# Two parts of a hybrid decoder's mixer trade places: sparse heads first and in pairs, MLA and stick-breaking beside half of the output projection

## The chip, the cores and the metric

One core of a Trainium2 chip (trn2) runs the kernel. The metric is the device time of one execution in microseconds, as the median of several runs. Lower is better.

## The reference

A decoder trunk of two layers on 256 tokens of width 1024, in float32. Each layer computes:

```python
x = x + 0.5 * swiglu(rmsnorm(x, g1), w_gate1, w_up1, w_down1)        # 2816 wide
h = rmsnorm(x, g_mix) @ w_in                                        # 2354 columns, cut into head groups
o_mla = mla_attention(...)              # 6 heads, low-rank q and kv, rotary key, causal softmax
o_nsa = nsa_attention(...)              # 6 query heads in 2 groups: compressed, selected, window branches
o_sb  = stick_breaking_attention(...)   # 4 heads, no softmax, strictly causal
x = x + concat(o_mla, o_nsa, o_sb) @ w_out                          # 1024 x 1024
x = x + 0.5 * swiglu(rmsnorm(x, g2), w_gate2, w_up2, w_down2)
```

and a last RMSNorm follows. With 256 tokens the selected and the window branch of the sparse attention (NSA) see all earlier tokens, so each is a plain causal softmax with keys and values of its own. The compressed branch has 15 keys and values per group, made by a two-layer network with GELU from overlapping runs of 32 tokens. A sigmoid gate weighs each branch.

## The kernel before

The residual stream lies feature-major in `xT`, 128 features on the partitions by 256 tokens. Weight matrices stay float32 in HBM. They come in as `raw` tiles (four buffers), and `split` (L86) makes two halves of each, `wh` on ScalarE and `wl = raw - wh` on VectorE, in a format that TensorE multiplies in one pass. A product is three matmuls of halves (`mm3`, L222, and the inner loops of `ffn` and `project`). The products of the attentions are full float32; each of those shows as two records in the trace.

`mix(l)` (L742) is the stage between the two feed-forward networks. Its parts are Python generators whose `yield`s cut them into steps. `weave(g, h, n)` (L403) traces all steps of `g` with `n` steps of `h` after each, and `mixed` (L414) traces several generators in turn. The order of tracing is a priority: the compiler's scheduler takes it, but lets work that is ready by its own estimate pass work that isn't. On the chip each engine then issues strictly in that order.

In `mix`, `project` (L370) computes one block of columns of the input projection into two PSUM banks. The order is: A (MLA's latents; statistics of the norm behind it), SQ (stick-breaking queries and keys) with `latents` (L510) woven in, SV, `up_project` (L525, MLA's queries, keys and values from the latents). Then come K, Q and V, the sparse attention's columns, woven with MLA (`latent_attention`, L605), stick-breaking (L556) and, from Q on, `compressed` (L625). After that `sparse_attention` (L720) runs by itself, one head after the other: `softmax_pair` (L460) computes the scores of the two branches, the probabilities and their transposes, and `pv` (L505) multiplies them with the values. Last comes the output projection in two halves of its columns (`out_half`, L835), all 1024 rows of `w_out` in each.

A head has 64 features, so a score matmul uses 64 rows of the array and a value matmul 64 columns. The six query heads lie as two groups on partitions 0 to 63 and 64 to 127. The PSUM banks have four tags of two each: `a0`, `a1`, `g0`, `g1`.

In `compressed` the first layer of the small network is 16 matmuls per branch with 30 rows of result (L650 to L655), all to the same partitions.

Of the kernel before, what the change touches and what calls it, by code (L numbers as in the profile page):

```python
# [10 lines left out]
F32 = mybir.dt.float32  # L11
# [8 lines left out]
T = 256  # L20
# [11 lines left out]
NB = 15  # L32

# [9 lines left out]
def _shape_constants():  # L43
# [13 lines left out]
    return tab, np.concatenate([tri, -np.ones((128, 128), np.float32), bd.reshape(128, 128)], 1)  # L57
# [3 lines left out]
def trunk(ctx, tc, a, out):  # L61
# [64 lines left out]
    mats = con.tile([128, 384], F32, name="mats")  # L126
    negtri, negones, bdm = mats[:, 0:128], mats[:, 128:256], mats[:, 256:384].rearrange("p (j d) -> p j d", j=2)
    cosn, sinn = tab[:, :, 0:16], tab[:, :, 16:32]
# [16 lines left out]
    for m in (maskc, masks, kcbd, hidp, pcm):  # L145
        POOL.memset(m, 0.0)
# [43 lines left out]
    def norm_in(n, l, d):  # L190
# [6 lines left out]
        else:  # L197
            s = sb.tile([128, T], F32, name="sq", tag="sq", bufs=2)
            ACT.activation(s, xT[:, d], AF.Square)
# [151 lines left out]
    def finish(xt2, t, c, sm):  # L351
        """Final norm: the gain first, the token's scale once both halves are summed."""
        s = slice(c * 512, c * 512 + 512)
        y = xt2[:, t, s]
        o = sb.tile([128, 768], F32, name="o", tag="PT", bufs=2)[:, :512]
# [14 lines left out]
    def project(l, c0, c1, tag):  # L370
        """One block of columns of the input projection, as a list of steps and its two banks."""
# [31 lines left out]
    def weave(g, h, n):  # L403
        """All steps of g, with n steps of h after each."""
# [9 lines left out]
    def mixed(*gens):  # L414
        """The steps of several generators in turn."""
# [44 lines left out]
    def softmax_pair(tag, q, k, res, gate=None):  # L460
        """Causal softmax of two score streams; the probabilities transposed: [key, stream, query]."""
# [11 lines left out]
        P = sb.tile([128, 768], F32, name="P", tag="P", bufs=2)  # L473
# [3 lines left out]
        for i, p, x, n in ((1, p1, x1, 256), (0, p0, x0, 128)):  # L477
# [6 lines left out]
            if gate is not None:  # L484
                DVE.tensor_tensor(f[:, i], f[:, i], gate[:, i], op=OP.mult)
# [13 lines left out]
        pt = sb.tile([128, 768], F32, name="PT", tag="PT", bufs=2)  # L499
# [5 lines left out]
    def pv(po, j, v, pt, first, last):  # L505
        rows = slice(64 * j, 64 * j + 64)
        mm(po[rows, 0:256], v[0], pt[0], first, False)
        mm(po[rows, 128:256], v[1], pt[1], False, last)

    def latents(l, A, ch, cl):  # L510
        """Transposes of the latents, with their gains, as exact halves."""
        for b0, nb in ((0, 2), (2, 1)):
# [5 lines left out]
            for b in range(nb):  # L518
                g = gam("mla_q_norm", l, b) if b0 == 0 else gam("mla_kv_norm", l, 0)
                pb = p[:, b * T:b * T + T]  # L520
                ACT.activation(ch[:, b0 + b], pb, AF.Copy, scale=g)
                DVE.scalar_tensor_tensor(cl[:, b0 + b], pb, g, ch[:, b0 + b].bitcast(F32), op0=OP.mult, op1=OP.subtract)
            yield

    def up_project(l, A, ch, cl, lr, qm, km, vm):  # L525
# [6 lines left out]
        for t in range(2):  # L532
            s = slice(t * 128, t * 128 + 128)
            q, k = qm[t], km[t]
            for c in range(2):
                p = bank("g%d" % c)[:, :288]
                f = slice(c * 288, c * 288 + 288)
                for kk in range(2):
                    mm(p, ch[:, kk, s], wuq[kk][0][:, f], kk == 0, False)
                    mm(p, ch[:, kk, s], wuq[kk][1][:, f], False, False)  # L540
                    mm(p, cl[:, kk, s], wuq[kk][0][:, f], False, kk == 1)
                evac(c, q[:, 3 * c:3 * c + 3].rearrange("p h d -> p (h d)"), p, lr[:, t:t + 1])
            for c in range(2):
                p = bank("g%d" % c)[:, :384]
                f = slice(c * 384, c * 384 + 384)
                mm(p, ch[:, 2, s], wkv[0][:, f], True, False)
                mm(p, ch[:, 2, s], wkv[1][:, f], False, False)
                mm(p, cl[:, 2, s], wkv[0][:, f], False, True)
# [7 lines left out]
    def stick_breaking(SQ, SV):  # L556
# [30 lines left out]
        for h in range(4):  # L587
# [12 lines left out]
            pv(po, h % 2, [SV[:, t, h * 64:h * 64 + 64] for t in range(2)], (at[:, 0:256], at[:, 256:384]), True, True)  # L600
# [4 lines left out]
    def latent_attention(qm, km, vm):  # L605
        for pr in range(3):
# [13 lines left out]
            for s in range(2):  # L620
                pv(po, s, [vm[:, t, 2 * pr + s] for t in range(2)], pts[0][s], True, True)
# [3 lines left out]
    def compressed(l, NQ, kv):  # L625
        """Keys and values of the compressed branch, on the diagonals of kcbd and kv."""
# [322 lines left out]
```

## Time and profile before

| | |
|---|---|
| median of 3 runs | 1097.53 us (1097.26 to 1099.15) |
| span of the profiled execution, first to last instruction | 1095.3 us |
| TensorE busy | 1072.1 us (98%), 8023 matmul records |
| VectorE, ScalarE, GpSimd busy | 62%, 49%, 9% |
| mean granted TensorE clock | 0.981 |
| HBM traffic | 160 GB/s over the span |

The page gives no device time of the profiled execution beside its span; the median of the runs stands for it. Engines are named PE (TensorE matmul), PEld (its weight loads), DVE (VectorE), ACT (ScalarE), POOL (GpSimd). A record's duration in a timeline reaches into the next one's, since matmuls are pipelined; the distance between two starts is what a matmul takes from the stream.

### The profile page before, as it was taken

The page shows a single profiled execution, that of the slowest core. Times are in us where ns is not written, and L with a number is a line of the kernel's source. Part 1 is how long each engine was busy: PE and PEld are TensorE (multiplying, and loading weights), DVE is VectorE, ACT ScalarE, POOL GpSimd, SP SyncE. Part 2 cuts the span into 40 slices and gives each one's busy share as a digit, 9 for nine tenths or more (in the row PEclk, how much of TensorE's full clock was granted, in tenths as well). Part 3 has the DMA queues.
Part 4 walks back from the last instruction along what each step waited for, and adds up shares of the span by engine and source line. Part 5 has one row for each costly group of instructions (what it writes and reads, how often), then busy time and mean ns, then how long its engine had stood idle before and what let it go on. Part 6 is the DMA issues. An engine that isn't in the chain of part 4 may idle for free.

```text
span 1095.3 us, 19386 instructions
## 1 busy us (share of the span) xinstructions
PE 1072.1 (98%) x8023; PEld 1008.0 (92%) x8023; DVE 684.3 (62%) x1088; ACT 535.7 (49%) x906; POOL 99.6 (9%) x171
## 2 busy tenths in 40 slices
PE   7999999999999999999999999999999999999996
PEld 7999999888868999999999999998887699999996
DVE  6666666765655766666686666667656466666664
ACT  5544444655444544444464444447645455444443
POOL 2000000322211100000020000003411220000001
PEclk9999999999969999999999999999998799999999
DMA  9646455373402456464555646553633035546441
GB/s 293 222 156 230 151 197 185 108 221 111 154 1 78 158 189 208 144 226 168 179 169 178 221 141 216 182 171 113 214 122 111 1 116 192 190 157 230 158 151 39
DMA packets 127974, 176.65 MB, mean 161 GB/s; under 512 B 4119, under 2 KB 106765, under 8 KB 127885
## 3 DMA queue, kind: packets, MB, share of 16 engines
q1 hardware_dynamic: 127392, 174.82, 47.3%
q8 instruction: 63, 1.03, 0.4%
q10 hardware_dynamic: 492, 0.59, 0.2%
q14 instruction: 27, 0.21, 0.1%
HBM read 174.34 MB, written 1.05 MB: 160 GB/s over the span
## 4 chain that ended last, share of the span: by engine, by line
PE 45%; DVE 2%; POOL 1%; ACT 1%; issue 1%; POOLq 0%; DVEq 0%
PE bkg L286 22%; PE bka L84 18%; PE bkg L84 3%; DVE wl L92 1%; DVE xl L193 0%; PE bkg L494 0%; PE bkg L612 0%; POOL rt L448 0%; PE bkg L496 0%; PE bkg L498 0%; POOL rt L449 0%; DVE xT L345 0%; DVE xt L335 0%; ACT wh L91 0%; POOL qm L451 0%
## 5 line engine op out<-in xcount | busy, mean ns | idle before, releaser
L91 ACT ACTIVATE wh<-raw 128x1024 fp32r<-128x1024 f32 (+4 forms) x332 | 339.0, 1025 | 426.9 <-PE bkg L286 203.5
L92 DVE TENSOR_TENSOR wl<-raw,wh 128x1024 fp32r<-128x1024 f32 (+4 forms) x332 | 394.1, 1191 | 185.5 <-ACT wh L91 178.9
L286 PE MATMUL bkg<-xl,wh 128*128 128x256 f32 x1392 | 390.3, 280 | 1.3 <-DVE xl L193 1.3
L286 PE MATMUL bkg<-xh,wh 128*128 128x256 f32 x1392 | 390.3, 281 | 0.7 <-ACT wh L91 0.7
L286 PE MATMUL bkg<-xh,wl 128*128 128x256 f32 x1392 | 389.4, 280 | 0.8 <-DVE wl L92 0.8
L286 PEld LDWEIGHTS bkg<-xl,wh 128*128 128x128 f32 x1392 | 262.1, 188 | 2.4 <-DVE xl L193 1.7
L286 PEld LDWEIGHTS bkg<-xh,wh 128*128 128x128 f32 x1392 | 262.1, 188 | 1.9 <-ACT wh L91 0.9
L286 PEld LDWEIGHTS bkg<-xh,wl 128*128 128x128 f32 x1392 | 262.0, 188 | 1.0 <-DVE wl L92 1.0
L84 PE MATMUL bka<-hh,wl 128*128 128x256 f32 x528 | 149.1, 283 | 0.0
L84 PE MATMUL bka<-hh,wh 128*128 128x256 f32 x528 | 148.9, 283 | 0.2
L84 PE MATMUL bka<-hl,wh 128*128 128x256 f32 x528 | 149.0, 283 | 0.0
L84 PEld LDWEIGHTS bka<-hh,wh 128*128 128x128 f32 x528 | 100.5, 191 | 0.8 <-ACT hh L308 0.8
L84 PEld LDWEIGHTS bka<-hh,wl 128*128 128x128 f32 x528 | 100.8, 191 | 0.0
L84 PEld LDWEIGHTS bka<-hl,wh 128*128 128x128 f32 x528 | 100.7, 191 | 0.0
L200 POOL TENSOR_TENSOR ss<-ss,sq 128x256 f32<-128x256 f32 x35 | 29.5, 844 | 599.4 <-issue 362.8
L300 DVE TENSOR_TENSOR t<-bkg,rb 128x256 f32<-128x256 f32 x88 | 37.4, 424 | 55.1 <-PE bkg L286 53.3
L84 PE MATMUL bka<-wh,xh 128*128 128x384 f32 (+4 forms) x192 | 68.5, 357 | 0.0
L303 DVE TENSOR_TENSOR t<-bkg,rb 128x256 f32<-128x256 f32 x88 | 37.3, 424 | 47.3 <-PE bkg L286 47.3
L84 PE MATMUL bka<-wh,xl 128*128 128x384 f32 (+4 forms) x192 | 66.4, 346 | 0.0
L84 PE MATMUL bka<-wl,xh 128*128 128x384 f32 (+4 forms) x192 | 66.3, 346 | 0.0
L440 ACT ACTIVATE P<-bka,st 128x256 f32<-128x256 f32 (+1 forms) x72 | 29.4, 415 | 31.7 <-PE bkg L498 14.4
L305 DVE TENSOR_TENSOR t<-t,t 128x256 f32<-128x256 f32 x88 | 37.4, 425 | 9.1 <-DVE t L303 0.5
(233 smaller groups left out, 1286.9 us busy)
## 6 DMA issues: line engine op xcount, KB each, us to landing
raw<-in_ffn_w_down_dram SPq DMA_DIRECT2D x44, 1024.0 KB, 5.1
raw<-in_ffn_w_gate_dram SPq DMA_DIRECT2D x43, 1024.0 KB, 5.8
raw<-in_ffn_w_up_dram SPq DMA_DIRECT2D x43, 1024.0 KB, 5.2
raw<-in_w_out_dram SPq DMA_DIRECT2D x16, 512.0 KB, 4.3
raw<-in_w_in_dram SPq DMA_DIRECT2D x8, 768.0 KB, 4.2
raw<-in_w_in_dram SPq DMA_DIRECT2D x4, 1024.0 KB, 5.4
raw<-in_w_in_dram SPq DMA_DIRECT2D x4, 832.0 KB, 4.5
raw<-in_w_in_dram SPq DMA_DIRECT2D x4, 804.0 KB, 5.5
```

What stands on the lines that cost most here:

```text
L84: PE.matmul(o, l, r, start=start, stop=stop, skip_group_check=True)
L91: ACT.activation(hv, src, AF.Copy)
L92: DVE.tensor_tensor(lv, src, hv.bitcast(F32), op=OP.subtract)
L200: POOL.tensor_tensor(state["ss"], state["ss"], s, op=OP.add)
L286: args[0](*args[1:], **flags)
L300: DVE.tensor_tensor(gn, pg[:, :T], rb, op=OP.mult)
L303: DVE.tensor_tensor(un, pu[:, :T], rb, op=OP.mult)
L305: DVE.tensor_tensor(h, gn, un, op=OP.mult)
L440: state["last_exp"] = ACT.activation(*args, **kw).ins
```

## The change

- The projections come in the order K, Q, V, A, SQ, SV. K and Q run bare, `compressed` is woven into V, and its rest, the transposes of the sparse rows and `sparse_attention` are one chain (`nsa`) woven into A, SQ, SV and `up_project`.
- `sparse_attention` takes a head of either group together: their score matmuls alternate between the two row halves, into a bank each; their value matmuls alternate between the column halves (`pv` now takes a list of heads). The gates and all scaling of the probabilities are applied on VectorE and GpSimd.
- The first layer of the compression writes to four groups of 32 partitions in turn, and a matmul with a 0/1 matrix (`sel32`) adds the four and turns the result.
- The output projection is cut by its rows: the sparse heads' three blocks (`out_sparse`) run first, for the second half of columns (added to `xT` at once) and then for the first, with MLA and stick-breaking woven in; the other five blocks follow (`out_late`). The sparse heads' rows of `w_out` are loaded in pieces of 64 rows.
- The ScalarE table for exp and log is loaded at the start of `mix` instead of behind A's squares.

```diff
@@ compressed
-            ph = bank("g1")[:30, :128]
             for j in range(16):
-                mm(ph, R[:, j].rearrange("p g b -> p (g b)"), w1[:, j], j == 0, j == 15)
+                c = slice(32 * (j % 4), 32 * (j % 4) + 32)
+                mm(ph[c], Rk[:, j], w1[:, j], j < 4, j >= 12)
...
-            PE.transpose(p[:, :30], hr[:30], ident[:30, :30])
+            mm(p[:, :32], hr, sel32, True, True)
@@ pv
-    def pv(po, j, v, pt, first, last):
-        rows = slice(64 * j, 64 * j + 64)
-        mm(po[rows, 0:256], v[0], pt[0], first, False)
-        mm(po[rows, 128:256], v[1], pt[1], False, last)
+    def pv(po, heads, first, last):
+        rows = [slice(64 * j, 64 * j + 64) for j in range(2)]
+        for j, (v, pt) in heads:
+            mm(po[rows[j], 0:256], v[0], pt[0], first, False)
+        for j, (v, pt) in heads:
+            mm(po[rows[j], 128:256], v[1], pt[1], False, last)
@@ sparse_attention
+        def scores(rr, t):
+            n = 128 * (t + 1)
...
+            X = [bank("a1") for _ in range(2)]
...
+            for g in range(2):
+                mm(xs[g][:, :, 128 * t:128 * t + 128], identb, maskc, True, False)
+            for s in range(2):
+                for g in range(2):
+                    mm(xs[g][:, s], nT[rr][grp[g], 128 * t:128 * t + 128], nT[3 + s][grp[g], 0:n], False, True)
...
+            for g in range(2):
+                POOL.tensor_tensor(p[g], p[g],
+                                   f[:, g].rearrange("p (s o) -> p s o", o=1).to_broadcast([128, 2, n]), op=OP.mult)
...
+        scores(0, 1)
+        yield
+        scores(0, 0)
+        yield
+        yield from compressed_probs(nT, gt, pct)
+        for rr in range(3):
+            if rr < 2:
+                scores(rr + 1, 1)
+                yield
+            turned(rr)
+            yield
+            if rr < 2:
+                scores(rr + 1, 0)
+                yield
+            values(rr)
+            yield
@@ mix
+        with tc.issue_after(state["square"]):
+            state["table"] = ACT.preload_act_table_set("natural_log_exp_and_others").ins
...
+        p = run(project(l, C_K, C_V, "a0"))
...
+        p = run(project(l, C_Q, C_K, "a1"))
...
+        cmp = compressed(l, NQ, vbd)
+        p = weave(project(l, C_V, C_SQ, "a0"), cmp, 1)
...
+        nsa = chain(cmp, sparse_rows(), sparse_attention(NQ, nT, gt, vbd, pct))
+        p = weave(project(l, C_A, C_Q, "a0"), nsa, 2)
...
+        p = weave(project(l, C_SQ, C_SV, "a0"), nsa, 2)
...
+        p = weave(project(l, C_SV, C_END, "a0"), nsa, 2)
...
+        weave(up_project(l, A, ch, cl, lr, qm, km, vm), nsa, 2)
+        run(nsa)
+        attn = mixed(stick_breaking(SQ, SV), latent_attention(qm, km, vm))
...
+        late = (6, 7, 0, 1, 2)
...
+        weave(out_sparse(1, [bank("a0") for _ in range(2)], True), attn, 5)
+        acc0 = [bank("a0") for _ in range(2)]
+        weave(out_sparse(0, acc0, False), attn, 5)
         run(attn)
...
+        run(out_late(0, acc0, False))
+        run(out_late(1, [bank("a1") for _ in range(2)], True))
```

## Rows read from the trace of the kernel before

**Rows 1.** The page's first part: busy time, share of the span and instructions of each engine.
```profile
PE 1072.1 (98%) x8023; PEld 1008.0 (92%) x8023; DVE 684.3 (62%) x1088; ACT 535.7 (49%) x906; POOL 99.6 (9%) x171
```

**Rows 2.** The windows view: stretch and its length, then busy us and instructions of PE, PEld, DVE, ACT and POOL, then the granted clock, the DMA share and GB/s. In order: the mixer of layer 0 and of layer 1, the 5.4 us before the clock falls, the stretch at the lower clock in layer 0 and in layer 1, a stretch of MLA and stick-breaking, and all of these two with the projections K, Q and V. The last row is the sixth one's stretch again, for the instructions on tile `wh` alone.
```profile
201.65:360.68 159.03, 156.17 (x950) 131.27 (x949) 95.90 (x202) 83.78 (x198) 37.40 (x66) 0.94 0.34 107
740.40:897.92 157.52, 154.61 (x951) 130.28 (x950) 95.97 (x202) 83.83 (x198) 37.50 (x66) 0.95 0.35 111
298.30:303.70 5.40, 5.18 (x38) 4.56 (x38) 4.23 (x11) 2.75 (x10) 0.85 (x4) 1.00 0.22 75
303.70:324.40 20.70, 20.70 (x65) 13.08 (x64) 9.41 (x34) 7.13 (x30) 4.20 (x7) 0.51 0.00 1
843.45:860.10 16.65, 16.65 (x50) 10.09 (x50) 8.82 (x34) 6.50 (x26) 3.23 (x6) 0.50 0.00 0
255.30:261.40 6.10, 6.10 (x45) 4.79 (x42) 3.48 (x7) 3.37 (x6) 0.25 (x1) 1.00 0.41 152
237.37:298.30 60.93, 59.16 (x380) 49.87 (x378) 35.02 (x73) 30.93 (x69) 14.18 (x31) 1.00 0.46 144
...
255.30:261.40 6.10, 1.06 (x4) 0.49 (x3) 0.99 (x1) 0.87 (x1) 0.00 (x0) 1.00 0.41 152
```

**Rows 3.** The timeline of PE in the sparse attention of layer 0 at the full clock: start us, us, engine, line, operation, output and inputs, tile of the array, shape, records. A row merges records in sequence.
```profile
325.47 0.27 PE L84 MATMUL bka<-maskc,identb 128*128 128x256 bf16 x1
325.67 0.71 PE L84 MATMUL bka<-nT 64*128 64x128 f32 x4
326.31 0.44 PE L494 MATMUL bkg<-ident,P 128*128 128x128 f32 x2
326.59 0.27 PE L84 MATMUL bka<-maskc,identb 128*128 128x256 bf16 x1
...
327.85 1.51 PE L84 MATMUL bkg<-PT,NQ 128*64 128x256 f32 x8
329.29 0.44 PE L496 MATMUL bkg<-ident,P 128*128 128x128 f32 x2
```

**Rows 4.** The timeline of PE among MLA (`vm`, `qm`, `km`) and stick-breaking (`SV`), same columns.
```profile
255.86 0.88 PE L84 MATMUL bkg<-PT,vm 128*64 128x256 f32 x8
256.56 0.81 PE L84 MATMUL bkg<-t,SV 128*64 128x256 f32 x4
257.31 0.64 PE L612 MATMUL bkg<-ident,qm 128*96 128x128 f32 x4
257.79 0.60 PE L612 MATMUL bkg<-ident,km 128*96 128x128 f32 x4
```

**Rows 5.** The timeline of PE at the scores of an MLA pair, 96 rows deep.
```profile
244.50 1.03 PE L84 MATMUL bka<-mT 96*128 96x256 f32 x4
245.37 0.27 PE L84 MATMUL bka<-maskc,identb 128*128 128x256 bf16 x1
```

**Rows 6.** The timeline of PE in `compressed`: the first layer of one branch and the row after it, then the small products of the second layer and the row after those.
```profile
276.88 3.68 PE L84 MATMUL bkg<-raw,R 128*30 128x128 f32 x32
280.49 0.64 PE L612 MATMUL bkg<-ident,km 128*96 128x128 f32 x4
...
288.39 0.29 PE L84 MATMUL bkg<-hx,w 128*64 128x15 f32 x4
288.61 0.69 PE L84 MATMUL bkg<-w,hidp 128*128 128x64 f32 x4
```

**Rows 7.** The timeline of PE at the transposes of A, in layer 0 and in layer 1; in brackets the idle time before the row and what ended it.
```profile
215.07 0.66 PE L517 MATMUL bkg<-ident,A 128*128 128x128 f32 x4 [0.86 <-ACT A L428]
...
753.85 0.67 PE L517 MATMUL bkg<-ident,A 128*128 128x128 f32 x4 [0.90 <-ACT A L428]
```

**Rows 8.** The timeline of PE in projection K: the second and the last of twelve matmuls of a step, ten steps apart.
```profile
241.38 0.34 PE L84 MATMUL bka<-wl,xh 128*128 128x384 f32 x1
...
243.14 0.34 PE L84 MATMUL bka<-wh,xl 128*128 128x384 f32 x1
```

**Rows 9.** The timeline of ACT at the start of layer 0's mixer: the last square of the norm, and the table load.
```profile
206.58 0.42 ACT L199 ACTIVATE sq<-xT 128x256 f32<-128x256 f32 x1 [0.66 <-POOL ss L200]
...
217.38 1.28 ACT L757 ACT_TABLE_LOAD   x1
```

**Rows 10.** The timelines of PE, DVE, ACT and POOL along the chains of MLA and stick-breaking in layer 0. On PE: the wait for the rotated queries, a mask of stick-breaking, its triangle products. On DVE: the softplus, and the two copies of MLA's transposed probabilities. On ACT: an exponential of stick-breaking. On POOL: the last scaling of an MLA pair.
```profile
240.27 0.53 PE L612 MATMUL bkg<-ident,qm 128*96 128x128 f32 x3 [1.76 <-POOL qm L451]
...
243.32 0.28 PE L84 MATMUL bkg<-masks,identb 128*128 128x256 bf16 x1
...
251.32 1.04 PE L84 MATMUL bkg<-t,mats 128*128 128x256 f32 x6
...
246.18 0.55 DVE L581 SCALAR_TENSOR_TENSOR t<-bkg,t 128x384 f32<-128x384 f32 x1
...
253.77 0.41 DVE L436 COPY PT<-bkg 128x256 f32<-128x256 f32 x1
255.03 0.69 DVE L436 COPY PT<-bkg 128x512 f32<-128x512 f32 x1 [0.85 <-PE bkg L498]
...
252.62 0.50 ACT L440 ACTIVATE t<-bkg 128x384 f32<-128x384 f32 x1
...
248.69 0.61 POOL L490 TENSOR_TENSOR P<-P,f 128x256 f32<-128x256 f32 x1 [0.48 <-DVE f L483]
```

**Rows 11.** The DMA view: issues, KB each, median us from issue to landing.
```profile
raw<-in_w_out_dram SPq DMA_DIRECT2D x16, 512.0 KB, 4.3
```

More of the change, by code (lines that the diff above doesn't have):

```diff
@@ L32 @@
 NB = 15
+PTB = 2
 def _rope_tables(rot):
@@ L144, in trunk @@
     pcm = con.tile([128, 2, 6, 32], F32, name="pcm")
-    for m in (maskc, masks, kcbd, hidp, pcm):
+    Rk = con.tile([128, 16, 32], F32, name="Rk")
+    for m in (maskc, masks, kcbd, hidp, pcm, Rk):
         POOL.memset(m, 0.0)
@@ L599, in stick_breaking @@
             yield
-            pv(po, h % 2, [SV[:, t, h * 64:h * 64 + 64] for t in range(2)], (at[:, 0:256], at[:, 256:384]), True, True)
+            pv(po, [(h % 2, ([SV[:, t, h * 64:h * 64 + 64] for t in range(2)], (at[:, 0:256], at[:, 256:384])))], True, True)
             if h % 2 == 1:
@@ L744, in mix @@
+        NQ = sb.tile([128, 2, 1298], F32, name="NQ", tag="NQ")
+        heads = [NQ[:, t, 0:1280].rearrange("p (h d) -> p h d", d=64)[:, :, 0:16] for t in range(2)]
+        vbd = sb.tile([128, 2, 2, 64], F32, name="vbd", tag="vbd")
+        p = run(project(l, C_K, C_V, "a0"))
         r = rstd_col()
@@ new lines, in prod, with halves @@
+        def prod(acc, e, W, d, first, last):
+            o = acc[d // 2][:, (d % 2) * T:(d % 2) * T + T]
+            w = (W[0][:, d * 128:d * 128 + 128], W[1][:, d * 128:d * 128 + 128])
+            mm3(o, w, (oh[:, e], ol[:, e]), first and d % 2 == 0, last)
+        def halves(raw, n):
+            W = []
+            for j in range(0, n, 2):
+                k = min(2, n - j)
+                h, lo = split(raw[:, j:j + k], 512 * k, "p (j f) -> p j f", j=k)
+                W += [(h[:, i], lo[:, i]) for i in range(k)]
+            return W
@@ new lines, in add, with out_sparse @@
+        def add(acc, c, dd):
+            x = xT[:, 4 * c + dd]
+            DVE.tensor_tensor(x, acc[dd // 2][:, (dd % 2) * T:(dd % 2) * T + T], x, op=OP.add)
+        def out_sparse(c, acc, stop):
+            W = halves(weights(c, (3, 4, 5)), 3)
+            for j in range(3):
+                for d in range(4):
+                    prod(acc, 3 + j, W[j], d, j == 0, stop and j == 2)
+                yield
+            if stop:
+                for d in range(4):
+                    add(acc, c, d)
+                yield
@@ new lines, in out_late @@
+        def out_late(c, acc, first):
+            W = halves(weights(c, late[:3]), 3) + halves(weights(c, late[3:]), 2)
+            for j in range(4):
+                for d in range(4):
+                    prod(acc, late[j], W[j], d, first and j == 0, False)
+                yield
+            for d in range(4):
+                prod(acc, late[4], W[4], d, False, True)
+                if d % 2 == 1:
+                    for dd in (d - 1, d):
+                        add(acc, c, dd)
+                        norm_in("ffn2_norm", l, 4 * c + dd)
+            yield
```

260 lines of the change are left out of this document (128 added, 132 removed).

## The prediction

> **What bounds the kernel now.** I read the page's busy row first: TensorE is busy for 1072.1 of 1095.3 us, VectorE for 62%, ScalarE for 49% and GpSimd for 9% [rows 1]. TensorE issues in order, so the time is the length of its stream: a change pays by what it takes out of that stream, or by a higher clock under it, and costs what it adds in waits of TensorE. The second view is the windows by stage, which also have the clock: the mixers take 159.03 and 157.52 us, and the rest of the kernel is untouched by the change [rows 2]. Inside them the clock is at its lower level (0.50 to 0.51, that is 1.2 GHz) for 20.70 us in layer 0 and 16.65 us in layer 1, with TensorE busy throughout; that is the sparse attention alone. It fell after 5.40 us (298.30 to 303.70) that held only turns of the sparse rows and narrow matmuls, with TensorE busy for 5.18 us; so what ran before the fall was thin work, not idleness. One thin stretch kept the full clock: 6.10 us of MLA and stick-breaking, with only four wide projection matmuls among them, 1.06 us [rows 2]. The third view, the timeline of TensorE, gives the price of each piece as the distance from one start to the next (a record's own duration overlaps its neighbour's).
>
> The sum is made on the profiled span, 1095.3 us. The median of the runs is 1097.53 us, so 2.2 us lie around the span; I carry them over.
>
> **The change part by part,** per layer, at the full clock first.
>
> *Scores in row halves.* A head now pays 326.31 - 325.47 = 0.84 us for a mask and the four 128-column records, and 327.85 - 326.59 = 1.26 us for a mask and the four 256-column ones [rows 3]: six heads, 12.6 us. Afterwards there are three pairs of heads, each with twice the records and still four masks in all. The mask's share is 0.20 us a time (325.47 to 325.67). No row shows two row halves abreast. If they don't overlap, a pair costs 0.8 + 2 x 0.64 + 2 x 1.06 = 4.2 us: nothing saved. If they overlap fully, 0.8 + 0.64 + 1.06 = 2.5 us: 7.5 us, saved 5.1. If the other half also hides the weight loads, a record costs what the 96-row one costs, (245.37 - 244.50)/4 = 0.22 us [rows 5], and some 0.11 at half the columns: 2.1 us a pair, saved 6.3. I take 5.1, since the column halves below do overlap.
>
> *Value products in column halves.* Eight records of one head's two branches take 329.29 - 327.85 = 1.44 us [rows 3]. The same eight records for two MLA heads, whose outputs lie in different halves, take 256.56 - 255.86 = 0.70 us [rows 4]: the overlap exists in this trace. Six groups: 8.6 us before, 4.2 after, saved 4.4. The shuffled order of `pv` changes nothing for MLA, which already has 0.70; the ends are 3.9 and 4.6.
>
> *Compression in column quarters.* The 32 records of one branch take 280.49 - 276.88 = 3.61 us, two branches 7.2 [rows 6]. Four abreast would be 0.9 a branch; the closest spacing of small records here is (288.61 - 288.39)/4 = 0.055 us, which gives 1.76; serial is 3.61. I take 1.76, the row that is nearest in form: saved 3.7, with ends 0 and 5.4. The full-width product that replaces the small turn of `hr` costs perhaps 0.15 us twice (an estimate: one more record at about the spacing of a compression record, 0.11, and some switch): 3.4 net.
>
> *The sparse work among the projections.* Its steps now lie between those of three dense projections instead of in a block. The dense matmuls themselves don't change in number. If the clock stays up, the low stretches halve: 10.35 us in layer 0 and 8.3 in layer 1 [rows 2]. The two savings above are at full-clock prices, so nothing is counted twice. The price if this fails is the whole term.
>
> *The wait for A goes.* TensorE idled 0.86 us in layer 0 and 0.90 in layer 1 for the eviction of A behind the row statistics [rows 7]. Now the same statistics come after the first projection, and the second one goes to other banks and needs neither: saved 0.9. Next late would be the compression's turns, which have the second projection, 48 matmuls of 0.176 us (243.14 - 241.38 over ten steps [rows 8]), 8.4 us, in front of them.
>
> *The ScalarE table load moves ahead of the mixer.* It takes 1.28 us; before it stood after A's squares. It now stands behind the last square of the norm [rows 9], and behind it queue the halves of the second projection, for which VectorE and then TensorE wait. The ends are 0 (they are some steps ahead) and 1.3; I take 0.4.
>
> *One pair of banks for four projections in a row.* V, A, SQ and SV all go to "a0", so each waits for the eviction of the last. Sparse steps cover it. Without that cover each of three borders costs about the 0.86 us of the wait above: 0 to 2.6, taken 1.
>
> *MLA and stick-breaking beside half of the output projection.* Before, they had the three dense projections around them and the stage had hardly an idle moment: 60.93 us, 59.16 busy, 1.76 of the idle time waiting for GpSimd's rotation of qm [rows 2, 10]. Taking away 132 dense matmuls at about 0.178 (23.5), the compression (7.2 and an estimated 2.5 for its small pieces) and that wait leaves some 26 us for the two attentions. Now they have 72 products of the output projection under them; at the kernel's mean of 1072.1/8023 = 0.13 us a record [rows 1] that is some 9 us, and later products can fill in as their heads finish. Against 35 us of TensorE work stand the chains. MLA, per pair of heads: from the scores at 244.50 to the last scaled probability at 248.69 + 0.61 is 4.8 us, the copies of the turned probabilities (253.77 to 255.03 + 0.69, some of it waiting) up to 2.0, the products 0.7, the next pair's turns 257.79 + 0.60 - 257.31 = 1.1 and their copy 0.7: 9.3 us, three pairs 28 [rows 4, 5, 10]. Stick-breaking, per head: mask to the end of softplus, 243.32 to 246.18 + 0.55, 3.4 us; triangles and exponential, 251.32 to 252.62 + 0.50, 1.8; products 257.31 - 256.56 = 0.75: 6 us, four heads 24, partly two deep. Side by side they are shorter than the 35 us. But both use the "g0" banks, and TensorE stands in order behind whichever is late. I take 3 us of new waits, with ends 0 and 8 (a third of the MLA chain uncovered). The qm wait stays about as it is: fewer dense matmuls stand in front of it.
>
> *Moved at no cost.* The weights of the output projection come in 22 smaller transfers a layer instead of 8 of 512 KB; the bytes are the same, the old ones landed in 4.3 us [rows 11], and the queue stood idle through the low stretches (DMA share 0.00 [rows 2]), so the load buffers cover them; without cover, one such landing a tile. GpSimd takes over ScalarE's share of the scaling: at 0.61 us per 128x256 [rows 10] three pairs cost 3 x 6 x 0.61 = 11 us, under a stage of some 50.
>
> Of switching between whole and divided array the trace has the 0.20 us from a mask to the first 64-row record. The Trainium skill, "TensorEngine Tiling (Array Packing)", section Key Properties, says that a change of tiling mode drains TensorE; this speaks against weaving divided pieces into whole-array projections. By it each extra cut would cost up to those 0.2 us, and ten more cuts a layer would take 4 us off the gain over both layers; the sum leaves them out because the score blocks fall from twelve to six. The same skill's "TensorE: Matmul & The Clock Gate", Part 3, gives 3.07 times for four row tiles; by it two halves would be near the overlapping end, and no row here shows it.
>
> **Sum.** Layer 0: -10.35 - 5.1 - 4.4 - 3.4 - 0.9 + 0.4 + 1 + 3 = -19.75 us; layer 1: -17.7. Together -37.4: span 1057.9, time 1060.
>
> **Rivals.**
> 1. *More of it works:* weights hidden, four quarters abreast, no new waits. Per layer 6.3 + 4.6 + 5.1 + 0.9 and the clock: -27.2 and -25.2, time 1045. For it: 0.70 against 1.44 us. Against: waits always came where stages were shortened.
> 2. *Row halves don't overlap:* +5.1 a layer, 1070. For it: no row shows them. Against: their results go to separate banks, and columns do overlap.
> 3. *The low clock moves to MLA and stick-breaking,* whose dense share falls from 23.5 of 61 us to 9 of 35. If it lasts as long as now, +18.7: 1079. For it: the fall came with TensorE busy, after thin work. Against: the 6.10 us at clock 1.00.
> 4. *The change doesn't do what it says:* the compiler still issues the sparse work in one block. The low stretches then shrink only with the work, by about a third, so some 12 us of the clock term are lost: 1072.
> 5. *Slower:* the shortened stage runs as a chain in series on the in-order TensorE: 28 us of MLA and 24 of stick-breaking one after the other, 52 us against 35 of work, 17 idle; and with the idle time the clock falls for the whole stage, another 35. That is 52 a layer, against the 3 allowed for: +98 in all, 1158. It turns the result to slower from 22 us a layer on, that is, when the chains add up and the clock falls for a quarter of the work. For it: two bank pairs shared. Against: the stage of before overlapped them.
>
> **How the numbers follow.** Forecast 0.48 (its own range 1051 to 1068), rival 1 0.15, rival 2 0.10, rival 3 0.13, rival 4 0.08, rival 5 0.06. A run tells 0.2%, 2.2 us, from no change. All but rival 5 are faster by more; of that one most is slower: faster 0.93, same 0.01, slower 0.06. From 1045 to 1081 some 0.17 is left out: rival 5, half of rival 1 and the ends of 3.
>
> **What would show it.** Right: score records of two halves starting together; 16 value records in about 1.4 us; 32 compression records in under 2 us; clock 1.00 through the sparse steps; mixers of some 139 us. Wrong: a stretch at 0.50 anywhere in the mixer; idle TensorE time above 8 us between the last up-projection and the last product; scores in the same time as before.

## The result and the profile after

The changed kernel takes 1066.26 us (median of 4 runs, 1064.5 to 1068.09) against 1097.39 for the kernel before in the same comparison: ratio 0.9723, 95% interval 0.9684 to 0.9761. It is faster, by 31 us where 37 were forecast; the profiled execution took 1064.5 us with a span of 1062.7, 32.6 less than before.

Two lines of the page of the changed kernel, its busy row and the group of the feed-forward products that read xl, and then the waits for xl before the change (releaser, sum in us, times, longest):

```profile
PE 1034.6 (97%) x8027; PEld 980.7 (92%) x8027; DVE 681.0 (64%) x1066; ACT 534.7 (50%) x912; POOL 109.2 (10%) x172
...
L290 PE MATMUL bkg<-xl,wh 128*128 128x256 f32 x1392 | 390.6, 281 | 3.5 <-DVE xl L197 3.5
```

```profile
PE bkg L286 <- DVE xl L193: 1.3, 1, 1.3
```

The windows of the changed kernel, columns as in [rows 2]: the two mixers, four microseconds in layer 0's, and what lies behind each mixer.

```profile
201.20:342.02 140.82, 137.44 (x952) 117.84 (x951) 92.01 (x188) 83.08 (x200) 41.14 (x66) 0.99 0.39 123
723.33:863.96 140.63, 136.01 (x952) 116.75 (x951) 92.13 (x188) 83.10 (x200) 41.08 (x66) 1.00 0.40 127
293.10:297.10 4.00, 3.66 (x16) 3.01 (x17) 0.91 (x2) 0.58 (x1) 0.84 (x2) 0.57 0.27 95
342.02:723.33 381.31, 377.82 (x3182) 376.18 (x3181) 246.64 (x342) 181.46 (x253) 11.72 (x14) 1.00 0.54 182
863.96:1062.70 198.74, 189.17 (x1344) 177.10 (x1342) 123.68 (x171) 90.93 (x130) 8.30 (x9) 0.99 0.47 159
```

TensorE has 37.5 us less to do, and the low stretches of 20.70 and 16.65 us [rows 2] are gone but for 3.4 us in layer 0. The mixers lost 18.21 and 16.89 us. The stretches behind them, whose matmuls the change does not alter, became longer, 381.31 from 379.72 and 198.74 from 197.38 (before: the distance between its mixers, and from its second mixer to the end of its span): 2.95 us, of which 2.2 are the new waits for xl. The mixer starts 0.45 us earlier. -18.21 - 16.89 + 2.95 - 0.45 = -32.6.

The timeline of TensorE in the changed mixer: 32 records of the compression and the row behind them, two blocks of scores, 16 value products and the row behind them, a third block of scores and the row behind it. A block is the scores of one pair of heads for one half of the tokens, eight records; it is issued as a pair when the records of the two row halves alternate.

```profile
224.09 1.08 PE L86 MATMUL bkg<-raw,Rk 128*32 128x128 f32 x32 [0.40 <-DVE Rk L651]
225.10 0.45 PE L86 MATMUL bka<-wh,xh 128*128 128x402 f32 x1
...
247.72 0.71 PE L86 MATMUL bka<-nT 64*128 64x128 f32 x4
248.35 0.50 PE L86 MATMUL bka<-wh,xh 128*128 128x512 f32 x1
248.70 0.28 PE L86 MATMUL bka<-maskc,identb 128*128 128x256 bf16 x1
248.91 0.71 PE L86 MATMUL bka<-nT 64*128 64x128 f32 x4
...
255.97 0.71 PE L86 MATMUL bka<-nT 64*128 64x128 f32 x8
256.61 1.52 PE L86 MATMUL bkg<-PT,NQ 128*64 128x256 f32 x16
258.06 0.70 PE L86 MATMUL bkg<-pct,vbd 64*128 64x256 f32 x2
...
261.92 1.13 PE L86 MATMUL bka<-nT 64*128 64x256 f32 x8
262.99 0.33 PE L767 MATMUL bkg<-ident,P 128*128 128x128 f32 x1
```

Eight score records of 256 columns take 262.99 - 261.92 = 1.07 us, as four did [rows 3]; eight of 128 take 0.64: the row halves overlap fully. Sixteen value products take 1.45, and 32 compression records 1.01 us where 1.76 was put in the sum. But the block at 247.72 was not issued as a pair: four records, a wide projection product and a mask, and only then the other four. Two of a layer's six blocks came out so.

### The profile page after: what moved, and what is told of

It reads as the page before. It is cut to its first block, busy times and chain, and to the rows that moved or that the text cites. A ratio compares the mean times of both kernels' runs of the same rounds, so it can differ in the third digit from the quotient of the medians.

```text
span 1062.7 us, 19409 instructions
## 1 busy us (share of the span) xinstructions
PE 1034.6 (97%) x8027; PEld 980.7 (92%) x8027; DVE 681.0 (64%) x1066; ACT 534.7 (50%) x912; POOL 109.2 (10%) x172
## 5 line engine op out<-in xcount | busy, mean ns | idle before, releaser
L93 ACT ACTIVATE wh<-raw 128x1024 fp32r<-128x1024 f32 (+5 forms) x336 | 339.3, 1017 | 407.3 <-PE bkg L290 205.9
L94 DVE TENSOR_TENSOR wl<-raw,wh 128x1024 fp32r<-128x1024 f32 (+5 forms) x336 | 397.0, 1186 | 185.6 <-ACT wh L93 178.3
L309 DVE TENSOR_TENSOR t<-t,t 128x256 f32<-128x256 f32 x88 | 37.4, 425 | 9.1 <-DVE t L307 0.5
L312 ACT ACTIVATE hh<-t 128x256 fp32r<-128x256 f32 x88 | 36.8, 418 | 8.4 <-DVE t L309 8.2
```

Of the source, the lines that this page charges most:

```text
L93: ACT.activation(hv, src, AF.Copy)
L94: DVE.tensor_tensor(lv, src, hv.bitcast(F32), op=OP.subtract)
L309: DVE.tensor_tensor(h, gn, un, op=OP.mult)
L312: ACT.activation(hh, h, AF.Copy)
```

## Which part does it: order and halves taken apart

**The order alone.** Two runs split the change. The first keeps the new order and puts the old sparse attention into it.

```diff
-            ph = bank("g1")[:, :128]
+            ph = bank("g1")[:30, :128]
             for j in range(16):
-                c = slice(32 * (j % 4), 32 * (j % 4) + 32)
-                mm(ph[c], Rk[:, j], w1[:, j], j < 4, j >= 12)
+                mm(ph, R[:, j].rearrange("p g b -> p (g b)"), w1[:, j], j == 0, j == 15)
...
-            X = [bank("a1") for _ in range(2)]
+            yield from softmax_pair("a1", [q, q], [nT[3][rows], nT[4][rows]], pts, gt[:, :, h, 1:3])
```

> The changed kernel's order, but with the sparse attention, the value products and the compression of the kernel before: one head at a time, no halves of rows, no alternating column halves, no quarters. Theory (the two parts add up): clock 1.00 throughout the sparse steps, scores with their masks some 12.6 us a layer (9.8 in the changed kernel), value products 8.6 (4.5), compression records 7.2 (2.0): 12 us a layer more than the changed kernel, time 1088 to 1092, so that the order alone is worth 5 to 10 us and the halves the rest. Rival 1 (longer thin pieces between the projections let the clock fall again): stretches at 0.5 in the mixers, time 1095 or more. Rival 2 (the projections hide part of what the halves save): time 1075 or less.

It took 1094.91 us, ratio 0.9986 (0.9962 to 1.0011): nothing that can be told from no change, and 3 us above the theory's range, though the clock did what the theory said. Its mixers in the windows view:

```profile
201.96:356.10 154.14, 150.77 (x950) 127.10 (x949) 96.65 (x206) 83.58 (x200) 40.10 (x66) 1.00 0.35 113
737.47:892.55 155.08, 151.08 (x950) 126.98 (x949) 96.99 (x206) 83.50 (x200) 39.38 (x66) 1.00 0.36 115
```

The clock is 1.00 throughout, and still the mixers are only 4.9 and 2.4 us shorter than before. The distances from one TensorE start to the next, added up by kind of work over layer 0's mixer (us; up to the start of its last product), say where the clock's gain went:

```
                            before   order alone   changed
scores                       14.96      10.19        6.88
their masks                   3.45       3.03        2.92
value products, sparse        9.87       8.67        4.50
turned probabilities          7.35       5.77        5.63
compression, first layer      7.34       7.33        2.02
output projection            23.32      24.87       25.14
scores of MLA, stick-br.      7.25       8.02        8.28
dense projections            54.97      55.62       54.50
idle                          2.86       3.37        3.38
all other                    27.54      27.15       27.46
```

From the first column to the second the sparse kinds give 9.3 us with the small ones (layer 1: 7.5). The output projection, the scores of the two other attentions, the dense projections and idle time take 3.5 of it back, and with smaller kinds 4.4. Behind the two mixers another 3.3 us were lost (381.37 and 199.05 us, from 379.72 and 197.38), as in the changed kernel. From the second column to the third the halves and quarters give 13.3 us (layer 1: 14.4).

**The halves in a block.** The second run keeps the halves and quarters and the new sequence of the projections and the output projection. All sparse work, compression included, runs as one block behind the up-projections. This is not the kernel before with halves put in: there the compression stood among other work.

```diff
-        p = weave(project(l, C_A, C_Q, "a0"), nsa, 2)
+        p = run(project(l, C_A, C_Q, "a0"))
...
-        p = weave(project(l, C_SQ, C_SV, "a0"), nsa, 2)
+        p = run(project(l, C_SQ, C_SV, "a0"))
...
-        p = weave(project(l, C_SV, C_END, "a0"), nsa, 2)
+        p = run(project(l, C_SV, C_END, "a0"))
...
-        weave(up_project(l, A, ch, cl, lr, qm, km, vm), nsa, 2)
+        run(up_project(l, A, ch, cl, lr, qm, km, vm))
```

> The changed kernel with its halves and quarters, but with the sparse steps run as one block again after the up-projections instead of between the projections. Theory (the clock falls after thin work with TensorE busy, and what keeps it up is the dense matmuls in between): the block of some 23 us of sparse work per layer shows the lower clock after its first 5 us, for 10 to 18 us; the mixers get 7 to 12 us a layer longer than those of the changed kernel (140.8 and 140.6), time 1080 to 1090; scores of a pair still start together. Rival (the halves alone bring the clock up, since they make the thin stretch short): no stretch below 0.9 there, mixers within 3 us of the changed kernel's, time 1064 to 1072.

1098.89 us, ratio 1.0014 (0.9983 to 1.0044): worse than either theory said. Its windows in layer 0 (the end of the wait ahead of the block, and the block), its waits of TensorE there (releaser, sum, times, longest), and from its timeline a block of scores issued as a pair and the two halves of one that was not:

```profile
266.50:272.60 6.10, 0.12 (x2) 0.00 (x0) 5.64 (x15) 1.87 (x5) 4.36 (x6) 0.91 0.25 88
272.60:299.00 26.40, 24.54 (x96) 17.51 (x96) 10.96 (x36) 8.68 (x36) 6.44 (x8) 0.50 0.02 4
```

```profile
PE bkg L86 <- DVE hx L673: 6.0, 1, 6.0
PE bka L86 <- ACT P L444: 1.8, 1, 1.8
```

```profile
277.44 2.08 PE L86 MATMUL bka<-nT 64*128 64x256 f32 x8
...
281.65 1.22 PE L86 MATMUL bka<-nT 64*128 64x128 f32 x4
...
283.84 1.22 PE L86 MATMUL bka<-nT 64*128 64x128 f32 x4
```

The expectation had the scores of a pair start together; in four of the six blocks of a layer they did not. Even so, and at the low clock, scores, value products and compression take 20.71 us in layer 0 where they took 32.17 before, 11.5 less. It was given back: nothing lay beside the chain of the compression's second layer (6.0 us) and of the first softmax (1.8), so that idle time rose by 6.4 us; the cut-up output projection took 2.1 more; all other kinds, among them the small sparse pieces now at the low clock, 2.1. The clock was low for 27.3 us a layer instead of 20.7 and 16.7.

So neither run alone is faster than before by more than the noise, and both parts together give 31 us. Each part does save TensorE time. With the order alone, weaving, waits and the stretches behind the mixers take most of it back; in the block, waits and the low clock do. What halves that all run in pairs would give in the order of before was not measured.

**Thin work or the long wait?** The 6.0 us of idle time come before that fall, so a third run moved only the attention of the three pairs into a block.

```diff
-        nsa = chain(cmp, sparse_rows(), sparse_attention(NQ, nT, gt, vbd, pct))
+        nsa = chain(cmp, sparse_rows())
+        att = sparse_attention(NQ, nT, gt, vbd, pct)
...
         run(nsa)
+        run(att)
```

> The changed kernel with its compression and the turns of the sparse rows still between the projections, and only the attention of the three pairs as one block after the up-projections (in the run that moved everything, the block began with a wait of 6.0 us, so that its low clock could come of the wait as well as of the thin work). Theory (thin work without dense matmuls lowers the clock, also with TensorE busy): no wait above 2 us ahead of the fall, and the block, some 18 us of work, at 0.50 for 10 us or more; mixers 6 to 12 us a layer longer than those of the changed kernel, time 1078 to 1092. Rival (only the long wait did it): the clock stays above 0.9 up to the first wait of a us or more, mixers within 3 us, time under 1073.

1084.66 us (two runs), ratio 0.9882 (0.9845 to 0.9919): some 13 us faster than before, with mixers of 150.70 and 145.34 us and idle time of 1.8 and 3.7 us in them, now that the compression is covered again. Its windows: the block at the low clock in layer 0, the low part in layer 1, and the 10.2 us behind that; then the row of TensorE's timeline at which the clock falls in layer 0.

```profile
272.00:296.00 24.00, 23.91 (x83) 15.48 (x83) 11.27 (x30) 9.53 (x42) 7.67 (x9) 0.50 0.08 23
...
808.00:814.80 6.80, 6.75 (x20) 4.14 (x19) 4.75 (x11) 3.24 (x14) 3.89 (x4) 0.50 0.17 62
814.80:825.00 10.20, 10.18 (x70) 7.16 (x70) 5.70 (x16) 5.57 (x24) 3.22 (x4) 1.00 0.00 1
```

```profile
272.08 0.37 PE L86 MATMUL bka<-maskc,identb 128*128 128x256 bf16 x1 [0.88 <-ACT P L444]
```

Layer 0 goes as the theory has it, with a wait of only 0.88 us ahead of the fall. Layer 1 does not: the same block had the low clock for 6.8 us, and then the full clock through 10 us of the same thin work. So a long wait isn't needed, and thin work alone doesn't decide it either; what does beyond that is open.

## The waits that were left

**Pairs that were not issued as pairs.** Two of the six score blocks of a layer ran one half after the other. This run chains the score products in the written order.

```diff
...
+                if last is None:
+                    last = mm(*a).ins
+                else:
+                    with tc.issue_after(last):
+                        last = mm(*a).ins
```

> The changed kernel with the score matmuls of each block of a pair chained in the written order, the two row halves alternating. In the changed kernel two of the six blocks of a layer ran one half after the other (starts of their records not in pairs). Theory (the halves overlap whenever they are issued alternately, and the two blocks lost it by the order of issue): all six blocks start in pairs, scores 5.1 to 5.4 us a layer instead of 6.88, mixers 1.2 to 1.8 us a layer shorter, time 2 to 4 us less than the changed kernel. Rival (the first half was issued early because the other bank was not yet free, so the chain only waits for it): scores shorter but idle time longer by as much, mixers within 0.5 us.

The scores fell to 5.20 us a layer, as the theory had it, and the time did not: 1068.68 us, ratio 0.974 (0.9716 to 0.9764), mixers 144.20 and 141.85. One view of its waits, in layer 0 right behind the first pair, where the changed kernel waits 0.3 us in all:

```profile
PE bkg L777 <- POOL P L759: 1.2, 2, 0.6
```

The turns of the probabilities now stand waiting for GpSimd's scaling; idle time grew by 1.4 and 1.3 us, which is nearly the 1.7 that the scores gained. That is what the rival says. Its mixers, within 0.5 us, did not come: they are 3.4 and 1.2 us longer than the changed kernel's, with 10.2 us of low clock behind the wait for qm in layer 0 (3.4 there) and 3.4 in layer 1 (none there).

**The wait for qm.** The prediction let it stand "about as it is". The timelines of the changed kernel, TensorE and then GpSimd:

```profile
291.23 0.27 PE L617 MATMUL bkg<-ident,qm 128*96 128x128 f32 x1
293.44 0.75 PE L617 MATMUL bkg<-ident,qm 128*96 128x128 f32 x3 [1.93 <-POOL qm L455]
...
290.39 0.60 POOL L453 TENSOR_TENSOR rt<-qm,tab 128x192 f32<-128x192 f32 x1
290.94 0.71 POOL L452 TENSOR_TENSOR rt<-A,tab 128x32 f32<-128x32 f32 x1
291.61 1.23 POOL L453 TENSOR_TENSOR rt<-A,tab 128x32 f32<-128x32 f32 x1
292.80 0.58 POOL L455 TENSOR_TENSOR qm<-rt,rt 128x192 f32<-128x192 f32 x1
```

Between qm's multiplies and qm's add GpSimd does two for A, which was ready long before.

```diff
+        for t in range(2):
+            rope(A[:, t:t + 1, 384:416], cosm[:, t], sinm[:, t], 16, 1, o=km[t][:, :, 64:96], no=6)
...
-            rope(A[:, t:t + 1, 384:416], cosm[:, t], sinm[:, t], 16, 1, o=k[:, :, 64:96], no=6)
```

> The changed kernel with the rotation of A's 32 columns written ahead of the up-projection's loop, so that GpSimd does not have it between qm's multiplies and qm's add. Theory (the wait of 1.93 and 1.94 us for qm is that of the two multiplies for A ahead of its add, 1.94 us together, and the low clock of 3.8 us in layer 0 comes of that wait): the wait falls under 0.5 us, no stretch at 0.5 is left, mixers 1.5 to 2 us shorter in layer 1 and 2.5 to 4 in layer 0, time 4 to 6 us less. Rival (qm's own multiplies end as late, or another chain is late next): the wait only changes its place, mixers within 0.7 us.

The wait is gone in both layers, and with it the low clock of layer 0: mixer 138.44, that is 2.4 us less. Time 1061.96 us, ratio 0.9675 (0.9657 to 0.9693). In layer 1 the mixer is 141.42, 0.8 more; the wait for the compression's rows was longer there:

```profile
PE bkg L86 <- DVE Rk L652: 2.0, 1, 2.0
```

and 3.4 us of low clock lie right around it. The additions that make Rk stand on VectorE behind a weight split, and that had waited for ScalarE's half of a weight block, for which ScalarE had waited 3.73 us on the load.

**The start of the second feed-forward.** Before, TensorE lost 1.3 us in all to waits for xl; the page of the changed kernel has 3.5, with 1.14 and 1.06 us at the starts of the second feed-forwards. Two blocks of the output projection were put together for each quarter at the end, as before the change:

```diff
-            for j in range(4):
+            for j in range(3):
...
             for d in range(4):
+                prod(acc, late[3], W[3], d, False, False)
                 prod(acc, late[4], W[4], d, False, True)
```

> The changed kernel with the last two row blocks of the output projection done together for each quarter of the output at the end, 24 matmuls per quarter as before the change instead of 12. Theory (the waits at the start of the second feed-forward, 2.7 us over both layers, come of too little TensorE work behind the last evictions): the two waits for xl fall to under 0.3 us each, time 2 to 2.5 us less. Rival (VectorE has a weight split of 1.76 us ahead of the last two parts of xl, whatever TensorE does): the waits stay within 0.3 us, time the same.

The waits at these starts are 1.21 us each, so they stayed, as the rival says, but the time was 1073.26 us, ratio 0.9778 (0.9744 to 0.9811), which neither says. In the profile all of it is the clock: low for 13.7 and 10.2 us behind the wait for qm, on instructions that are those of the changed kernel.

**All three edits together** (the three diffs above, no other line changed):

> The three edits of the runs e3, e4 and e5 together. If each of them does what its theory says and they add up, 8 to 11 us less than the changed kernel: 1055 to 1058. If the rivals hold throughout: 1064 to 1067. If only the pairs and the rotation work: 1058 to 1061.

1065.88 us, ratio 0.9713 (0.9692 to 0.9734). The chained scores made TensorE wait 1.0 and 0.6 us for the scaled probabilities in both layers, with 3.4 us of low clock behind; that took back what the rotation gave. It lies where all the rivals together put it, 1064 to 1067.

**Is the length of a low stretch set by the program?** The changed kernel and the run with the tail moved were run again, with nothing edited.

> The changed kernel once more, nothing edited. In its first profile the same wait of 1.93 and 1.94 us for qm, with the same instructions behind it, was followed by 3.4 us of low clock in layer 0 and none in layer 1, and in the run with the tail moved by 13.7 and 10.2 us. Theory (how long the clock is low behind that wait is not set by the program, it differs from one execution to the next): the waits are the same to 0.02 us, the low stretches are not, the rest of the mixers agrees to 0.5 us, and the time goes with the low stretches, 1062 to 1075. Rival (the program sets it): again 3.4 us in layer 0 and none in layer 1, mixers 140.8 and 140.6.

> The run with the tail moved once more, nothing edited. Its TensorE instructions around the wait for qm are those of the changed kernel, yet it had 13.7 and 10.2 us of low clock behind that wait, and the changed kernel 3.4 and 0 in both of its profiles. Theory (chance of the execution): other lengths this time, time 1064 to 1072. Rival (something that the edit moved, as the moment at which the stretch begins, sets it): again 10 us or more in each layer, time 1070 to 1077.

The changed kernel took 1070.72 us (1064.58 to 1075.48), ratio 0.9751 (0.9716 to 0.9787), with 3.4 us and none again in its mixers (141.07 and 140.62), which is what the rival said of them, but 6.8 us of low clock in the feed-forwards at 542, where its first profile had none. The run with the tail took 1066.55 us, ratio 0.9742 (0.9707 to 0.9778). Its two profiles, in the windows behind the wait for qm, the first execution and then the second:

```profile
293.80:308.20 14.40, 14.07 (x52) 11.84 (x53) 2.72 (x7) 6.32 (x18) 2.05 (x4) 0.53 0.09 31
823.00:833.60 10.60, 10.60 (x38) 8.74 (x38) 2.50 (x6) 5.14 (x15) 1.23 (x2) 0.53 0.23 73
```

```profile
293.50:307.90 14.40, 14.20 (x99) 11.94 (x100) 7.56 (x17) 8.79 (x22) 1.92 (x4) 1.00 0.15 42
816.00:826.60 10.60, 10.60 (x76) 9.48 (x75) 5.16 (x13) 7.33 (x19) 1.48 (x3) 1.00 0.22 75
```

One program, the same wait of 1.93 to 1.94 us: 52 matmul records in 14.4 us in one execution and 99 in the other. The two profiles come from two chips; but the four runs on the second chip alone spread from 1063.74 to 1072.58 us, with mean clocks of 0.998 and 0.988. So the length differs from one execution to the next. Differences of a few us between these kernels' medians are therefore read from their mixers and waits, not from the medians alone.

**MLA and stick-breaking without the products between them.** From here on the edits start from the run with the rotation moved.

```diff
-        weave(out_sparse(1, [bank("a0") for _ in range(2)], True), attn, 5)
+        run(attn)
+        run(out_sparse(1, [bank("a0") for _ in range(2)], True))
```

(and the second woven call likewise)

> The run with the rotation moved, but with MLA and stick-breaking without the 72 products of the output projection per layer between their steps (these follow as a block). Theory (these products keep the clock up and cover the chains of the two attentions): the stage of some 26 us of work shows 0.50 over most of its length and idle time of 4 us or more, mixers 8 to 18 us a layer longer, time 1078 to 1098. Rival (the two attentions cover each other, and the products only cost their changes of tile mode): no low stretch above 4 us, the output projection 22.5 to 23.5 us instead of 24.9, mixers within 3 us, time 1058 to 1066.

1064.50 us, ratio 0.9698 (0.9677 to 0.9719); mixers 140.17 and 139.35, near the rival. But it did not test what it was made for: in the trace products of the output projection still stand between the steps, since the compiler fills the places where an attention waits. They cost 26.0 us, not 22.5. The wait for qm came back (1.96 us), with fewer products ahead of it. Whether bare attentions would lose the clock stays open.

**A version that is faster than the changed kernel.** One more projection step before the compression's products:

```diff
             yield
+            yield
             ph = bank("g1")[:, :128]
```

> The run with the rotation moved, and in addition one more step of the dense projection between the turns of the compressed rows and the products of each compression branch. Theory (the one wait left at the compression, 1.99 us in layer 1, is that of its additions behind a late weight split on VectorE, and the low clock of 3.4 us there comes of it): the wait falls under 0.5 us in both layers, no stretch below 0.9 is left in either mixer, mixers 138.0 to 138.5 in both layers instead of 138.4 and 141.4, time 1057 to 1060. Rival (each step given to one chain takes it from the next, as when the pairs were chained): another wait of 1 us or more appears, mixers no shorter than 138.4 and 141.4, time 1061 to 1065.

1060.15 us (1059.28 to 1063.12), ratio 0.9663 (0.9645 to 0.9681). Its mixers:

```profile
202.16:339.30 137.14, 135.13 (x952) 116.49 (x951) 92.22 (x188) 83.32 (x200) 40.28 (x66) 1.00 0.40 127
721.75:859.60 137.85, 135.46 (x953) 116.32 (x951) 92.28 (x188) 83.23 (x200) 39.44 (x66) 1.00 0.41 129
```

No wait above 0.4 us is left in them, and no stretch below full clock: 6.5 us less than the changed kernel's two mixers. The last run, on top of that one, tried the start of the second feed-forward once more, now from VectorE's side:

```diff
...
+                after = state["xl"] if f == 1 and not first else None
-                G = split(rg[:, :, o:o + 128], 1024, "p (k f) -> p k f", k=KD)
+                G = split(rg[:, :, o:o + 128], 1024, "p (k f) -> p k f", after=after, k=KD)
...
```

> The run with the rotation moved and the later compression products, and in addition the weight splits of the second row block of each feed-forward held behind the last part of xl on VectorE. Theory (what remains of the waits at the start of the second feed-forward, 1.16 and 1.15 us, is the split of 1.76 us that VectorE does ahead of the last two parts of xl): these waits fall under 0.4 us, time 1 to 3 us less than that run's, 1057 to 1059. Rival (the split that was held back is late next, a wait of about as much one block later): time within 0.7 us of that run's.

1065.45 us, ratio 0.9707 (0.9682 to 0.9731). The waits for xl are gone; in layer 0 two others took their place,

```profile
PE bkg L225 <- POOL r L218: 1.3, 1, 1.3
PE bkg L295 <- DVE wl L96: 1.2, 1, 1.2
```

each as long, and 3.4 us of low clock follow in both layers. The time is 5.3 us more than without this edit, which neither theory nor rival had. Holding the splits back only moved the waits; whether another order on VectorE would end them was not tried.

## Why the prediction was right, and where its sum was not

**Clock term.** Right in kind, too large: -10.35 and -8.3 per layer were half of the low stretch; the run with the order alone measured -9.3 and -7.5. Not every record at the low clock was twice as long: in layer 0, 16 value products before the change took 4.10 us there (319.92 to 324.02), and twice 1.44 is their price at the full clock [rows 3]. That the clock stays up once dense products lie between was right in the profile of that run, and but for 3.4 us in that of the changed kernel.

**Halves.** The sum had -5.1 - 4.4 - 3.4 = -12.9 a layer; scores, value products and compression together gave 12.8 in layer 0 against the order alone (the mixers differ by 13.3 and 14.4). That the total fits is in part luck: scores 1.8 less than put, compression 1.9 more. The scores gave only 3.3 of 5.1, because two blocks were not issued as pairs; the chained run had 5.0 and paid it back as waits. The value products gave 4.2 of 4.4. The compression gave 5.3, near the far end of 5.4: the quarters do run four abreast. The row halves overlap fully, eight records in the time of four. The Trainium skill's "TensorE: Matmul & The Clock Gate", Part 3, gives 3.07 times the speed for four row tiles. The two halves measured here come to 2.0 times.

**What had no price: the weaving.** The sum set nothing for switching between whole and divided array, "because the score blocks fall from twelve to six". But the output projection was now cut up too, among products of 96 rows, of 64 rows and of 64 columns: 1.55 us more in layer 0 of the order-alone run and 1.8 in the changed kernel (with its 3.4 us of low clock), and 0.8 more in the scores of MLA and stick-breaking. Over both layers these are some 5 us. Three places of the changed kernel's timeline at the full clock, a cut by two turns, the way into products of 64 columns and the way out:

```profile
303.03 0.38 PE L496 MATMUL bkg<-ident,P 128*128 128x128 f32 x2
303.17 0.37 PE L86 MATMUL bka<-oh,wh 128*128 128x256 f32 x1
303.37 0.28 PE L86 MATMUL bka<-ol,wh 128*128 128x256 f32 x1
...
305.94 0.28 PE L86 MATMUL bka<-oh,wh 128*128 128x256 f32 x1
306.15 0.87 PE L86 MATMUL bkg<-PT,vm 128*64 128x256 f32 x8
...
310.68 0.38 PE L86 MATMUL bka<-ol,wh 128*128 128x256 f32 x1
310.90 0.28 PE L86 MATMUL bka<-oh,wl 128*128 128x256 f32 x1
```

In an uncut run a product of the output projection takes 0.12 us and two turns 0.22. A cut by two turns, which use the whole array, costs nothing: turns and first product take 0.34 together. Ahead of products of 64 columns the last one takes 0.21, and the first one behind such products 0.22: some 0.1 us for each change. (The 0.20 us that the prediction read from a mask to the first score record holds the mask's own 0.1, as at 299.30 to 299.40 of the kernel before.) The Trainium skill's "TensorEngine Tiling (Array Packing)", Key Properties, says that a change of tiling mode drains TensorE. This case's trace agrees that such a change has a price, where the sum had none; the prediction's estimate by that rule, 4 us, was near in size.

**The waits.** A's wait went, as said. The new waits of 3 + 1 us a layer did not come in that stage: idle time in the mixer rose by 0.5 and 1.7 us in all, with the waits for qm and, in layer 1, Rk as its largest pieces. The 2.95 us behind the mixers were not in the sum, which took the rest of the kernel as untouched; VectorE does a split of 1.76 us there ahead of the last xl.

**How the total came near.** The terms for waits, banks and the table, -0.9 + 0.4 + 1 + 3 a layer, put 7.0 us on the time where idle time rose by 2.2. That makes room for most of what stood at nothing: -37.4 + 1.9 (clock) + 4.6 (weaving, from the order-alone run) - 4.8 + 2.95 - 0.45 = -33.2, measured -32.6. So the mechanisms of the large terms were right, and the closeness of the sum owes something to errors that cancel. The second four runs of the same kernel had their median at 1070.72 us, outside the forecast's own range of 1051 to 1068. And one sign of being wrong did come, a stretch at 0.50 in a mixer, if only for 3.4 us.

**Rivals.** Rival 1 was right on the quarters; its waits of nothing and scores beyond full overlap did not come. Row halves overlap, so 2 falls. The compiler wove the steps in, so 4 falls. Rival 3 came in a small way: the low clock did move to MLA and stick-breaking, for 3.4 us, behind a wait, and in one execution of the run with the tail moved for 13.7. The chains did not add up, so 5 falls.

## What to carry to other kernels

Halving the work of an engine pays in time only as far as the chains that feed it are covered: in the block here 11.5 us of shorter work in a layer went into waits, the price of the new order and small pieces at the low clock. And cover has a price of its own: count each place where whole-array products are cut by products of 64 rows or columns, some 0.1 us on the way in and as much on the way out. Take away the waits of one to two us inside thin stretches first: they cost their own length, and in some executions 3.4 to 13.7 us of low clock followed them.

## What the runs showed of the hardware that was not expected

The length of a low-clock stretch is not a property of the program alone: between 0 and 13.7 us behind one and the same wait, in a kernel whose runs took 1063.7 to 1076.4 us, the longer ones at lower mean clocks (0.998 to 0.985). Ten microseconds of thin work at full clock, in the run with only the attention in a block, stand beside 24 us of the same work at half. And four column quarters run so nearly together that a record costs 1.01/32 = 0.03 us instead of 0.11.
